# A recurrent layer whose operands are normalised ahead of its products, in token halves of 384 and 256

## The chip, the core and the metric

The kernel runs on one core of one Trainium2 chip. The metric is the device time of one execution in microseconds; the median of three runs of the kernel before is 1546.01 us (1545.75 to 1546.52). Engines are named as in the profile: PE (TensorE) with its weight loads PEld, DVE (VectorE), ACT (ScalarE), POOL (GpSimd) and SP, which issues most DMAs.

## The reference, cut to what matters

One step of a two-layer backbone over 512 latent tokens and 128 context tokens of width 1024, in float32. Layer 0 is attention and an FFN; layer 1 is a gated linear recurrent unit and an FFN. Every sub-layer starts with an RMS norm and a shift and scale that differ for latent and context tokens. The change touches the end of layer 0's FFN and the recurrent unit:

```
def _modulate(x, g, shift, scale):
    return _rms_norm(x, g) * (1 + scale[:, None, :]) + shift[:, None, :]

gate, xr = jnp.split(xm @ w_in, 2, axis=-1)           # two products, 1024 x 1024 each
xc = _centred_depthwise_conv(xr, conv_w, conv_b)      # 4 taps, zeros outside the sequence
a, b = _rglru_coeffs(xc, ...)                         # per direction: sigmoid, exp, sqrt
y = (scan_forward + scan_backward) * gelu(gate)
out = x + g * (y @ w_out)
```

## The kernel before, in words

Activations lie with features on the 128 partitions, eight feature tiles `k` by 640 tokens (512 latent tokens, stored column by column of the grid, then 128 context tokens). Each float32 operand is split into a rounded high part and a low part, and a product of one weight unit (eight 128x128 tiles, one output tile `f`) is three matmuls per `k`: hi x hi, hi x lo, lo x hi (`chunk`, lines 213 to 215). A product's result lies in one PSUM bank; the layer has three banks `mm` for them, and two pairs `gp` for the small gate products of line 1003.

**Last projection.** `project` multiplies for each `f` in token halves of 320, adds the result to the residual stream `x` (`residual`, L436), squares it for the statistics (L375, L377), and at once writes `x * A` as the next layer's operands `nh`, `nl` (`scale`, L419, L420): these are scaled but not normalised. After the last `f`, `stats` computes each token's mean square and its inverse root (`moment`: L389, L392, `var` L394, `rs` L396 on POOL, `dg` L398) and spreads it over the partitions (`spread`, L406), copied into `rt` (L430). `shift` puts the shift vector B into two further token columns, 640 and 641.

**Recurrent layer.** For each of eight feature tiles (columns, here) there are two products, `lru_xr` and `lru_gate`, in halves of 322 and 320 tokens (`CHB`): the two further columns give W B, copied to `bias` (L202). Eviction multiplies by `rt` on DVE (L981 for xr, written in row order of the grid; L1054 for the gate). Since W B is left to the bias, the pads of xr outside the sequence are filled with -bias (L973), and the convolution's constant `cbs` (L975) holds bias times the sum of taps. Then, per column, in the loop over `t` in `run`: `lru_a` (convolution L991, L993; small products L1003; tanh L1004; L1005), one step later `lru_b` (L1011; Exp L1015; tanh L1016; Sqrt L1017; L1018; L1019), one later `lru_c` (scans L1028; state L1030; sums L1035, L1036), and `lru_d` (gelu L1041; product with y L1042; high part L1046, low part L1047). A column takes three of ten buffers `lt` (`tr`, `ti`, `a`); `y` lives in `a`. The gate product of column f stands in the same step as its `lru_d`, but for column 0, which stands in the first step.

**What sets the order.** Engines run their own queues in order. Which instruction comes next on a queue is fixed at compile time by a planner: in a simulated run with its own costs, each engine takes the ready instruction that stands earliest in the program. Weights (`unit`): SP loads the float32 unit into one of three buffers `raw`; in the recurrent layer POOL loads it a second time straight into the high part `whi` (L178, three buffers), and DVE subtracts for `wlo` (L182). In the FFN phase there are three further buffers `whx`, `wlx`, and every second unit takes one of these. The output projection that follows (`project_halves`) needs the operands of all eight columns for its first product.

Of the kernel before, what the change touches and what calls it, by code (L numbers as in the profile page):

```python
# [9 lines left out]
F32 = mybir.dt.float32  # L10
F32R = mybir.dt.float32r
AF = mybir.ActivationFunctionType
# [113 lines left out]
class _Step:  # L126
# [313 lines left out]
    def project(self, w, hi, lo, gk, nxt=None, done=None, ahead=False):  # L440
        G = self.need(self.gcols, gk)
        for f in range(KT):
            u = self.unit(w[f], "m" if ahead else None)
            for t0, t1 in CH:
                self.residual(f, t0, t1, self.chunk(u, hi, lo, t0, t1, not ahead or f > 1), G, nxt)
                if nxt:
                    self.scale(f, t0, t1, *nxt)
            if done:
                done(f)
        if nxt:  # L450
            self.stats()
            self.shift(*nxt)

    def project_part(self, w, hi, lo, gk, also=None):
        G = self.need(self.gcols, gk)
# [465 lines left out]
    def lru_prep(self, pool):  # L921
        nc = self.nc
        c = CI["lam0"] * KT
        lam = self.t([P, 2 * KT], F32, "lam", 1, pool)
        nc.sync.dma_start(lam, self.i["cols"][:, c:c + 2 * KT])
        n = 2 * KT

        def sm(tag):
            return self.t([P, n], F32, tag, 1)
        ab = sm("l_ab")  # L930
        nc.vector.tensor_scalar(ab, lam, -1.0, None, ALU.mult)
        mx = sm("l_mx")
        nc.vector.tensor_scalar(mx, ab, 0.0, None, ALU.max)
        nc.vector.tensor_tensor(ab, ab, lam, ALU.min)
        y = sm("l_y")
        nc.scalar.activation(y, ab, AF.Exp)
        den = sm("l_den")
        nc.vector.tensor_scalar(den, y, 2.0, None, ALU.add)
        nc.vector.reciprocal(den, den)
        z = sm("l_z")  # L940
        nc.vector.tensor_tensor(z, y, den, ALU.mult)
        z2 = sm("l_z2")
        nc.vector.tensor_tensor(z2, z, z, ALU.mult)
        pl = sm("l_pl")
        nc.vector.memset(pl, 1.0 / 19)
        for c in range(17, 0, -2):
            nc.vector.tensor_tensor(pl, pl, z2, ALU.mult)
            nc.vector.tensor_scalar(pl, pl, 1.0 / c, None, ALU.add)
        nc.vector.tensor_tensor(pl, pl, z, ALU.mult)
        sp = sm("l_sp")  # L950
        nc.vector.scalar_tensor_tensor(sp, pl, 2.0, mx, ALU.mult, ALU.add)
        self.sp2 = sm("l_sp2")
        nc.vector.tensor_scalar(self.sp2, sp, 2.0, None, ALU.mult)
        self.sm4 = sm("l_sm4")
        nc.vector.tensor_scalar(self.sm4, sp, -4.0, None, ALU.mult)
        self.scw = self.t([P, KT], F32, "l_scw", 1)
        c = CI["cw0"] * KT
        nc.vector.tensor_reduce(self.scw, self.cols[:, c:c + 4 * KT].rearrange("p (j k) -> p k j", j=4), AX.X, ALU.add)
        self.hb = self.t([P, 4 * KT], F32, "l_hb", 1)
        c = CI["ba0"] * KT  # L960
        nc.vector.tensor_scalar(self.hb, self.cols[:, c:c + 4 * KT], 0.5, None, ALU.mult)

    def lru_xr(self, f, hi, lo, lp):
        nc = self.nc
        xr = self.t([P, 648], F32, "xr", 2, lp)
        nat = xr[:, 2:514].rearrange("p (r c) -> p c r", r=ROWS)

        def ev(t0, s, ps):
            if t0 == 0:
                todo = ((nat[:, 56:64], 0, 64, ROWS), (nat[:, 0:32], 64, 320, ROWS))  # L970
            else:
                for g, a, b in ((0, 0, 2), (0, 514, 515), (1, 515, 517), (1, 645, 646)):
                    nc.scalar.mul(xr[:, a:b], self.bias[:, g:g + 1].broadcast_to([P, b - a]), -1.0)  # L973
                self.cbs = self.t([P, 2], F32, "cbs", 2, lp)
                nc.vector.tensor_scalar(self.cbs, self.bias, self.scw[:, f:f + 1], self.col("cb", f), ALU.mult, ALU.add)  # L975
                todo = ((nat[:, 32:56], 320, 512, ROWS), (xr[:, 517:645], 512, 640, 0))
            for o, a, b, r in todo:
                v, w = ps[:, a - t0:b - t0], self.rt[:, a:b]
                if r:
                    v, w = [q.rearrange("p (c r) -> p c r", r=r) for q in (v, w)]  # L980
                nc.vector.tensor_tensor(o, v, w, ALU.mult)  # L981
        self.ws(self.i["wi"][KT + f], hi, lo, ev, ch=CHB)
        return xr, self.cbs

    def lru_a(self, f, xr, cbs, lp):
        nc = self.nc
        gw = self.t([P, 2, 2, P], F32, "gw", 2, lp)
        nc.sync.dma_start(gw, self.i["wg"][f])
        xc = self.t([P, LW], F32, "xc", 2, lp)
        for g, a, b in ((0, 0, NLAT), (1, NLAT, LW)):  # L990
            nc.scalar.activation(xc[:, a:b], xr[:, a:b], AF.Identity, scale=self.col("cw0", f), bias=cbs[:, g:g + 1])  # L991
        for j in range(1, 4):
            nc.vector.scalar_tensor_tensor(xc, xr[:, j:j + LW], self.col(f"cw{j}", f), xc, ALU.mult, ALU.add)  # L993

# [41 lines left out]
        nc.vector.tensor_tensor(y[:, NLAT:NTOK], h[:, 0, C0:LW], h[:, 1, C0:LW], ALU.add)  # L1036
        return y

    def lru_d(self, f, y, G, bias, yhi, ylo):
        for c, a, b in _pieces(0, NTOK):  # L1040
            self.nc.scalar.activation(G[:, a:b], G[:, a:b], AF.Gelu_apprx_tanh, bias=bias[:, c:c + 1])  # L1041
        self.nc.vector.tensor_tensor(y, y, G, ALU.mult)  # L1042
        self.split(yhi[:, f], ylo[:, f], y)

# [4 lines left out]
    def lru_gate(self, f, hi, lo, lp):  # L1049
        nc = self.nc  # L1050
        G = self.t([P, NTOK], F32, "gl", 3, lp)

        def ev(t0, s, ps):
            nc.vector.tensor_tensor(G[:, s], ps, self.rt[:, s], ALU.mult)  # L1054
        self.ws(self.i["wi"][f], hi, lo, ev, ch=CHB)
        return G, self.bias

    def new_x(self, st):
        pool = st.enter_context(self.tc.tile_pool(name="x", bufs=1))
# [6 lines left out]
    def run(self):  # L1066
# [65 lines left out]
        with self.phase("ffn0", at=2, rr=1, mx=2, wx=2, quota=56) as fp:  # L1132
            self.project(i["wo"], ohi, olo, (0, 2), ((0, 1), xhi, xlo), None, True)

            def last(w, hhi, hlo, gk):
                self.nh, self.nl = self.big(n=NTOK + 2), self.big(n=NTOK + 2)
                self.project(w, hhi, hlo, gk, ((1, 0), self.nh, self.nl),
                             lambda f: nc.sync.dma_start(xd[f * P:f * P + P], self.x[:, f]))
            self.ffn(0, xhi, xlo, fp, last)
        xpool.close()  # L1140
        mpool.close()
# [3 lines left out]
        ylo = self.big()  # L1145
        with self.phase("lru", at=1) as lp:
            A, B, C, G = {}, {}, {}, {}
            xr = self.lru_xr(0, xhi, xlo, lp)
            for t in range(KT + 2):
                if t < KT:  # L1150
                    A[t] = self.lru_a(t, *xr, lp)
                if t + 1 < KT:
                    xr = self.lru_xr(t + 1, xhi, xlo, lp)
                if 0 < t <= KT:
                    B[t - 1] = self.lru_b(t - 1, *A.pop(t - 1))
                if t > 1:
                    C[t - 2] = self.lru_c(t - 2, *B.pop(t - 2))
                g = 0 if t == 0 else t - 2
                if g > 0 or t == 0:
                    G[g] = self.lru_gate(g, xhi, xlo, lp)  # L1160
                if t > 1:
                    self.lru_d(t - 2, C.pop(t - 2), *G.pop(t - 2), yhi, ylo)
            nc.sync.dma_start(o["nh"], self.st)
        x1, x2 = self.big(n=NTOK + 2), self.big(n=NTOK + 2)
        self.new_x(self.ctx)
# [32 lines left out]
```

## Time and profile before

| | us |
|---|---|
| median of 3 runs (lowest, highest) | 1546.01 (1545.75, 1546.52) |
| the profiled execution | 1547.73 |
| its span, first to last instruction | 1546.0 |
| PE, DVE, ACT, POOL busy | 1492.0, 1069.5, 698.5, 215.9 |

Mean granted TensorE clock over the span: 0.988 of full speed. How to read it: PE's busy time is a union of modelled matmul spans, each longer than the distance to the next start, so short gaps don't show in it; DVE and ACT times are measured, and neighbouring instructions overlap by some 0.08 us. All times below are microseconds from the span's start unless marked ns. The last matmul of the last projection starts at 854.6, the recurrent layer's products begin at 855.1, and the output projection, which begins at 1025.6, waits before 1036.9.

### The profile page before, as it was taken

Reading aid. Unit: us, or ns where it says so; the run is one execution under the profiler, and the core shown is the slowest. Engines: PE = TensorE matmul, PEld = TensorE weight load, DVE = VectorE, ACT = ScalarE, POOL = GpSimd, SP = SyncE. Lnnn points to the kernel's source line nnn. Section 1 sums busy time; section 2 is a strip of 40 time slices with the busy share of each in tenths; the row PEclk is TensorE's granted clock in tenths of the full one; section 3 lists DMA queues with packets and bytes.
Section 4 is the critical chain, followed back from the end, with each engine's and each line's share of the span. In section 5 each row is a group of like instructions: output and inputs, shape, how many; then the busy total and the mean of one; then the engine's idle time right before and its main releaser. Section 6 shows DMA issues by size and latency. Waiting matters only on the chain. (4 is left out here: it accounts for less than half of the span.)

```text
span 1546.0 us, 26069 instructions
## 1 busy us (share of the span) xinstructions
PE 1492.0 (97%) x10315; PEld 1444.8 (93%) x10315; DVE 1069.5 (69%) x2034; ACT 698.5 (45%) x1304; POOL 215.9 (14%) x247
## 2 busy tenths in 40 slices
PE   6999999989999999999999999979999999999997
PEld 4899999879999999999999987869999999999996
DVE  5668788959998988443446479965875655555556
ACT  5576766655333113312324378762634342525242
POOL 2101122100111110000000000000222322222210
PEclk9999999999999999999999999989999999999998
DMA  9545656525566664222224433315242232323211
GB/s 373 151 117 162 188 165 174 154 105 186 190 193 192 188 208 140 62 82 82 65 73 133 131 115 106 103 55 201 79 130 82 83 96 69 96 69 93 72 56 68
DMA packets 72057, 196.64 MB, mean 127 GB/s; under 512 B 8048, under 2 KB 23552, under 8 KB 71808
## 3 DMA queue, kind: packets, MB, share of 16 engines
q1 hardware_dynamic: 57824, 144.49, 29.9%
q0 software_dynamic: 13824, 50.34, 10.8%
q8 instruction: 81, 1.33, 0.4%
q14 instruction: 40, 0.33, 0.1%
q10 hardware_dynamic: 288, 0.16, 0.0%
HBM read 179.48 MB, written 8.92 MB: 122 GB/s over the span
## 5 line engine op out<-in xcount | busy, mean ns | idle before, releaser
L213 PE MATMUL mm<-big,whi 128*128 128x320 f32 (+2 forms) x1290 | 402.8, 316 | 14.9 <-ACT big L1046 9.5
L214 PE MATMUL mm<-big,whi 128*128 128x320 f32 (+2 forms) x1290 | 405.6, 315 | 2.1 <-DVE big L1047 1.7
L215 PE MATMUL mm<-big,wlo 128*128 128x320 f32 (+2 forms) x1290 | 403.5, 314 | 0.7 <-DVE wlo L182 0.7
L213 PEld LDWEIGHTS mm<-big,whi 128*128 128x128 f32 x1290 | 245.3, 191 | 20.1 <-ACT big L1046 10.3
L214 PEld LDWEIGHTS mm<-big,whi 128*128 128x128 f32 x1290 | 246.5, 191 | 5.3 <-DVE big L1047 3.9
L215 PEld LDWEIGHTS mm<-big,wlo 128*128 128x128 f32 x1290 | 246.1, 191 | 2.2 <-DVE wlo L182 1.1
L243 DVE SCALAR_TENSOR_TENSOR mprod<-mraw,csb 128x1024 f32<-128x1024 f32 x160 | 195.6, 1223 | 14.6 <-DMA mraw<-in_wm 14.2
L436 DVE SCALAR_TENSOR_TENSOR x<-mm,G,x 128x128 f32<-128x128 f32 (+3 forms) x211 | 85.3, 434 | 86.1 <-PE mm L215 85.1
L182 DVE TENSOR_TENSOR wlo<-raw,whi 128x1024 fp32r<-128x1024 f32 (+1 forms) x90 | 110.5, 1228 | 33.4 <-ACT whi L180 21.1
L180 ACT CAST whi<-raw 128x1024 fp32r<-128x1024 f32 (+1 forms) x74 | 76.7, 1037 | 101.3 <-PE mm L214 69.6
L215 PE MATMUL mm<-big,wlx 128*128 128x320 f32 (+3 forms) x363 | 112.6, 310 | 0.0
L214 PE MATMUL mm<-big,whx 128*128 128x320 f32 (+3 forms) x363 | 112.3, 309 | 0.0
L213 PE MATMUL mm<-big,whx 128*128 128x320 f32 (+3 forms) x363 | 112.3, 309 | 0.0
L239 POOL DMA_DIRECT2D mraw<-in_wm x80 | 43.3, 542 | 385.0 <-DVE mprod L243 278.1
L213 PE MATMUL mx<-big,whi 128*128 128x320 f32 (+2 forms) x278 | 86.4, 311 | 0.9 <-DVE big L658 0.9
L215 PE MATMUL mx<-big,wlo 128*128 128x320 f32 (+2 forms) x278 | 86.1, 310 | 0.0
L214 PE MATMUL mx<-big,whi 128*128 128x320 f32 (+2 forms) x278 | 86.0, 309 | 0.0
L180 ACT CAST whx<-raw 128x1024 fp32r<-128x1024 f32 (+1 forms) x40 | 41.0, 1028 | 91.0 <-PE mm L214 53.3
L215 PE MATMUL mx<-big,wlx 128*128 128x320 f32 (+3 forms) x245 | 76.3, 311 | 0.0
L213 PE MATMUL mx<-big,whx 128*128 128x320 f32 (+3 forms) x245 | 76.1, 311 | 0.0
L214 PE MATMUL mx<-big,whx 128*128 128x320 f32 (+3 forms) x245 | 76.1, 311 | 0.0
L1046 ACT CAST whi<-raw 128x1024 fp32r<-128x1024 f32 (+1 forms) x41 | 41.3, 1008 | 71.3 <-PE mm L214 45.0
(292 smaller groups left out, 3589.0 us busy)
## 6 DMA issues: line engine op xcount, KB each, us to landing
raw<-in_gu SPq DMA_DIRECT2D x88, 512.0 KB, 3.6
mraw<-in_wm POOLq DMA_DIRECT2D x80, 512.0 KB, 4.0
raw<-in_dn SPq DMA_DIRECT2D x24, 512.0 KB, 3.6
raw<-in_wqk SPq DMA_DIRECT2D x16, 512.0 KB, 4.7
raw<-in_wi SPq DMA_DIRECT2D x16, 512.0 KB, 3.6
whi<-in_wi POOLq DMA_DIRECT2D x16, 512.0 KB, 3.9
raw<-in_dn SPq DMA_DIRECT2D x16, 448.0 KB, 3.4
sw<-in_wm SPq DMA_DIRECT2D x10, 512.0 KB, 10.4
```

The costliest lines, as they stand in the source:

```text
L180: nc.scalar.copy(hi, raw)
L182: nc.vector.tensor_tensor(lo, raw, hi.bitcast(F32), ALU.subtract)
L213: nc.tensor.matmul(ps, hi[:, k], xhi[:, k, s], start=(k == 0), stop=False)
L214: nc.tensor.matmul(ps, hi[:, k], xlo[:, k, s], start=False, stop=False)
L215: nc.tensor.matmul(ps, lo[:, k], xhi[:, k, s], start=False, stop=(k == nk - 1))
L239: nc.gpsimd.dma_start(w, self.i["wm"][l * 6 + j - 2, f])
L243: nc.vector.scalar_tensor_tensor(prod, w, 1.0, self.csb[:, s], ALU.mult, ALU.mult, accum_out=out[:, s, f:f + 1])
L436: self.nc.vector.scalar_tensor_tensor(xs, ps[:, a - t0:b - t0], G[:, s, f:f + 1], xs, ALU.mult, ALU.add)
L1046: self.nc.scalar.copy(hi, v)
```

## The change

- A new `project_closing` takes the place of `project` for the last projection of layer 0's FFN. All eight weight units are kept; the halves are 384 and 256 tokens (`CHL`). Tiles 0 and 1 are done in both halves, tiles 2 to 7 first in the first half alone. The statistics of the first half follow, then the second halves of tiles 2 to 7, and among them the first half is normalised, scaled, shifted and split (`modulate`: DVE, ACT, DVE for each piece); then the second half's statistics and the same for it. `x` is stored in two pieces per tile.
- The recurrent layer multiplies the normalised operands: no columns for B, no bias, no `rt`. xr is evicted by plain ACT copies; its pads are zeros, set once in two standing buffers; xc's first tap is one ACT instruction.
- The gate's first half is copied by ACT, its second half goes through gelu straight from PSUM, and the first half's gelu follows directly.
- The order at the start: first halves of xr 0, gate 0 and xr 1, then the second halves.

```diff
+    def project_closing(self, w, hi, lo, gk, key, nh, nl, xd):
+        G = self.need(self.gcols, gk)
+        A, B = [self.need(self.AB, key + (j,)) for j in range(2)]
+        us = []
+
+        def out(f, t0, t1):
+            self.residual(f, t0, t1, self.chunk(us[f], hi, lo, t0, t1), G, True)
+            self.nc.sync.dma_start(xd[f * P:f * P + P, t0:t1], self.x[:, f, t0:t1])
+
+        def normed(k, t0, t1):
+            v = self.t([P, 384], F32, "nv", 3, self.sb)
+            for s, a, b in _pieces(t0, t1):
+                self.modulate(k, a, b, A[:, s, k:k + 1], B[:, s, k:k + 1], v[:, a - t0:b - t0], nh, nl)
+        for f in range(KT):
+            us.append(self.unit(w[f]))
+            for c, (t0, t1) in enumerate(CHL):
+                if c == 0 or f < KT - DEH:
+                    out(f, t0, t1)
+        for c, (t0, t1) in enumerate(CHL):
+            for f in range(KT - DEH, KT) if c else ():
+                out(f, t0, t1)
+                j = f - KT + DEH
+                for k in range(max(0, 2 * j - 2), 2 * j) if f < KT - 1 else ():
+                    normed(k, *CHL[0])
+            self.stat(t0, t1)
+        for k in range(KT):
+            normed(k, *CHL[1])
...
+    def halves(self, w, hi, lo, ev):
+        u = self.unit(w)
+        return [lambda t0=t0, t1=t1: ev(t0, self.chunk(u, hi, lo, t0, t1)) for t0, t1 in CHL]
+
+    def lru_xr(self, f, hi, lo):
+        xr = self.xrs[f % 2]
         nat = xr[:, 2:514].rearrange("p (r c) -> p c r", r=ROWS)
-        def ev(t0, s, ps):
-            if t0 == 0:
-                todo = ((nat[:, 56:64], 0, 64, ROWS), (nat[:, 0:32], 64, 320, ROWS))
-            else:
-                for g, a, b in ((0, 0, 2), (0, 514, 515), (1, 515, 517), (1, 645, 646)):
-                    nc.scalar.mul(xr[:, a:b], self.bias[:, g:g + 1].broadcast_to([P, b - a]), -1.0)
-                self.cbs = self.t([P, 2], F32, "cbs", 2, lp)
-                nc.vector.tensor_scalar(self.cbs, self.bias, self.scw[:, f:f + 1], self.col("cb", f), ALU.mult, ALU.add)
-                todo = ((nat[:, 32:56], 320, 512, ROWS), (xr[:, 517:645], 512, 640, 0))
-            for o, a, b, r in todo:
...
-                nc.vector.tensor_tensor(o, v, w, ALU.mult)
+        def ev(t0, ps):
+            for o, a, b, r in ((nat[:, 56:64], 0, 64, ROWS), (nat[:, 0:40], 64, 384, ROWS),
+                               (nat[:, 40:56], 384, 512, ROWS), (xr[:, 517:645], 512, 640, 0)):
+                if t0 <= a and b <= t0 + 384:
+                    v = ps[:, a - t0:b - t0]
+                    self.nc.scalar.copy(o, v.rearrange("p (c r) -> p c r", r=r) if r else v)
+        return self.halves(self.i["wi"][KT + f], hi, lo, ev)
...
-        for g, a, b in ((0, 0, NLAT), (1, NLAT, LW)):
-            nc.scalar.activation(xc[:, a:b], xr[:, a:b], AF.Identity, scale=self.col("cw0", f), bias=cbs[:, g:g + 1])
+        nc.scalar.activation(xc, xr[:, 0:LW], AF.Identity, scale=self.col("cw0", f), bias=self.col("cb", f))
...
-    def lru_d(self, f, y, G, bias, yhi, ylo):
-        for c, a, b in _pieces(0, NTOK):
-            self.nc.scalar.activation(G[:, a:b], G[:, a:b], AF.Gelu_apprx_tanh, bias=bias[:, c:c + 1])
+    def lru_d(self, f, y, G, yhi, ylo):
         self.nc.vector.tensor_tensor(y, y, G, ALU.mult)
...
-        def ev(t0, s, ps):
-            nc.vector.tensor_tensor(G[:, s], ps, self.rt[:, s], ALU.mult)
-        self.ws(self.i["wi"][f], hi, lo, ev, ch=CHB)
-        return G, self.bias
+        def ev(t0, ps):
+            if t0 == 0:
+                nc.scalar.copy(G[:, 0:384], ps)
+                return
+            last = nc.scalar.activation(G[:, t0:NTOK], ps, AF.Gelu_apprx_tanh).ins
+            with self.tc.issue_after(last):
+                nc.scalar.activation(G[:, 0:t0], G[:, 0:t0], AF.Gelu_apprx_tanh)
+        return G, self.halves(self.i["wi"][f], hi, lo, ev)
...
-                self.project(w, hhi, hlo, gk, ((1, 0), self.nh, self.nl),
-                             lambda f: nc.sync.dma_start(xd[f * P:f * P + P], self.x[:, f]))
+                self.project_closing(w, hhi, hlo, gk, (1, 0), self.nh, self.nl, xd)
...
-            xr = self.lru_xr(0, xhi, xlo, lp)
+            self.xrs = [self.t([P, 648], F32, f"xr{j}", 1, lp) for j in range(2)]
+            for xr in self.xrs:
+                for a, b in ((0, 2), (514, 517), (645, 648)):
+                    nc.gpsimd.memset(xr[:, a:b], 0.0)
+
+            def gate(g):
+                G[g], halves = self.lru_gate(g, xhi, xlo, lp)
+                return halves
+            x0, g0, x1 = self.lru_xr(0, xhi, xlo), gate(0), self.lru_xr(1, xhi, xlo)
+            for step in (x0[0], g0[0], x1[0], x0[1], g0[1]):
+                step()
             for t in range(KT + 2):
                 if t < KT:
-                    A[t] = self.lru_a(t, *xr, lp)
+                    A[t] = self.lru_a(t, lp)
                 if t + 1 < KT:
-                    xr = self.lru_xr(t + 1, xhi, xlo, lp)
+                    for step in self.lru_xr(t + 1, xhi, xlo) if t else x1[1:]:
+                        step()
...
-                g = 0 if t == 0 else t - 2
-                if g > 0 or t == 0:
-                    G[g] = self.lru_gate(g, xhi, xlo, lp)
+                if t > 2:
+                    for step in gate(t - 2):
+                        step()
```

## Rows read from the trace of the kernel before

**Rows 1.** The page, part 1: busy us (share of the span) xinstructions.

```profile
PE 1492.0 (97%) x10315; PEld 1444.8 (93%) x10315; DVE 1069.5 (69%) x2034; ACT 698.5 (45%) x1304; POOL 215.9 (14%) x247
```

**Rows 2.** Stretches: us; busy (instructions) of PE, PEld, DVE, ACT, POOL; clock, DMA.

```profile
834.00:855.00 21.00, 21.00 (x145) 21.00 (x145) 12.63 (x27) 6.97 (x17) 1.05 (x2) 1.00 0.42 123
855.00:900.00 45.00, 43.82 (x278) 39.80 (x278) 19.78 (x38) 17.66 (x40) 3.88 (x6) 1.00 0.40 121
900.00:1003.00 103.00, 98.97 (x573) 85.85 (x572) 98.53 (x137) 84.38 (x136) 4.75 (x9) 0.98 0.36 110
1003.00:1028.00 25.00, 22.40 (x138) 21.59 (x137) 15.31 (x19) 22.34 (x27) 0.00 (x0) 0.93 0.16 44
1028.00:1041.00 13.00, 4.46 (x17) 3.80 (x16) 11.69 (x18) 2.71 (x7) 0.00 (x0) 0.67 0.11 38
```

**Rows 3.** Waits of PE, 855 to 1041: total us, times, longest us.

```profile
PE mm L213 <- ACT big L1046: 8.4, 1, 8.4
PE gp L1003 <- ACT lt L1004: 3.7, 3, 2.3
PE mm L213 <- DVE gl L1054: 2.9, 4, 1.9
```

**Rows 4.** Timeline of PE in the last product: start us, us, instruction.

```profile
1517.51 0.34 PE L215 MATMUL mm<-big,wlo 128*128 128x384 f32 x1
1517.68 0.28 PE L213 MATMUL mx<-big,whi 128*128 128x256 f32 x1
1517.80 0.28 PE L214 MATMUL mx<-big,whi 128*128 128x256 f32 x1
```

**Rows 5.** Groups by line, DVE, 860 to 1042: busy us, mean ns | idle before.

```profile
L182 DVE TENSOR_TENSOR wlo<-raw,whi 128x1024 fp32r<-128x1024 f32 x16 | 19.6, 1228 | 8.1 <-DMA whi<-in_wi 6.3 <-ACT whi L180 1.8
L981 DVE TENSOR_TENSOR xr<-mm,r 128x192 f32<-128x192 f32 (+3 forms) x32 | 10.8, 416 | 2.4 <-PE mm L215 2.4
L1054 DVE TENSOR_TENSOR gl<-mm,r 128x320 f32<-128x320 f32 x16 | 7.8, 499 | 0.7 <-PE mm L215 0.7
L975 DVE TENSOR_SCALAR cbs<-bias,l_scw,cols 128x2 f32<-128x2 f32 x8 | 2.3, 285 | 0.9 <-ACT bias L202 0.9
```

**Rows 6.** Groups by line, ACT, 860 to 1042.

```profile
L1041 ACT ACT_TABLE_LOAD x8 | 10.3, 1283 | 0.1
L1017 ACT ACT_TABLE_LOAD x8 | 10.3, 1283 | 0.1
L991 ACT ACTIVATE xc<-xr,cbs,cols 128x131 f32<-128x131 f32 (+1 forms) x16 | 9.8, 652 | 6.3 <-DVE xr L981 6.3
L973 ACT ACTIVATE xr<-bias 128x2 f32<-128x2 f32 (+1 forms) x32 | 3.8, 190 | 0.3 <-ACT r L430 0.2
L430 ACT COPY r<-rr 128x320 f32<-128x320 f32 x2 | 0.8, 425 | 4.9 <-PE rr L406 4.9
```

**Rows 7.** Groups by line and shape, DVE, 1490 to 1546 (the last projection of all).

```profile
L486 DVE SCALAR_TENSOR_TENSOR x<-x,cols,mx 128x384 f32<-128x384 f32 x8 | 4.5, 606 | 0.0
L436 DVE SCALAR_TENSOR_TENSOR x<-mm,G,x 128x128 f32<-128x128 f32 x10 | 3.1, 345 | 1.5 <-PE mm L215 1.5
L377 DVE TENSOR_TENSOR ssq<-ssq,sq 128x256 f32<-128x256 f32 x6 | 2.5, 422 | 1.3 <-ACT sq L375 1.1
```

**Rows 8.** Timeline of DVE at the statistics, 860 to 862.

```profile
860.20 0.23 DVE L394 TENSOR_SCALAR var<-at 128x3 f32<-128x3 f32 x2 [3.24 <-PE at L392]
861.42 0.56 DVE L398 TENSOR_TENSOR dg<-ident,rs 128x384 f32<-128x384 f32 x1 [0.99 <-POOL rs L396]
```

**Rows 9.** Timeline of DVE and of ACT at the layer's end.

```profile
1001.05 0.86 DVE L1047 TENSOR_TENSOR big<-lt,big 128x640 fp32r<-128x640 f32 x1
...
1023.60 1.50 DVE L1018 SCALAR_TENSOR_TENSOR lt<-lt,lt 128x1286 f32<-128x1286 f32 x1 [1.49 <-ACT bias L202]
...
1007.12 3.37 ACT L1015 ACTIVATE lt<-lt,l_sm 128x643 f32<-128x643 f32 x4
...
1010.40 0.78 ACT L1004 ACTIVATE lt<-gp,l_hb 128x643 f32<-128x643 f32 x1
```

More of the change, by code (lines that the diff above doesn't have):

```diff
@@ L955, in lru_prep @@
         nc.vector.tensor_scalar(self.sm4, sp, -4.0, None, ALU.mult)
-        self.scw = self.t([P, KT], F32, "l_scw", 1)
-        c = CI["cw0"] * KT
-        nc.vector.tensor_reduce(self.scw, self.cols[:, c:c + 4 * KT].rearrange("p (j k) -> p k j", j=4), AX.X, ALU.add)
         self.hb = self.t([P, 4 * KT], F32, "l_hb", 1)
@@ L961, in lru_prep, with lru_a @@
         nc.vector.tensor_scalar(self.hb, self.cols[:, c:c + 4 * KT], 0.5, None, ALU.mult)
-    def lru_xr(self, f, hi, lo, lp):
-        nc = self.nc
-        xr = self.t([P, 648], F32, "xr", 2, lp)
-        nat = xr[:, 2:514].rearrange("p (r c) -> p c r", r=ROWS)
-        def ev(t0, s, ps):
-            if t0 == 0:
-                todo = ((nat[:, 56:64], 0, 64, ROWS), (nat[:, 0:32], 64, 320, ROWS))
-            else:
-                for g, a, b in ((0, 0, 2), (0, 514, 515), (1, 515, 517), (1, 645, 646)):
-                    nc.scalar.mul(xr[:, a:b], self.bias[:, g:g + 1].broadcast_to([P, b - a]), -1.0)
-                self.cbs = self.t([P, 2], F32, "cbs", 2, lp)
-                nc.vector.tensor_scalar(self.cbs, self.bias, self.scw[:, f:f + 1], self.col("cb", f), ALU.mult, ALU.add)
-                todo = ((nat[:, 32:56], 320, 512, ROWS), (xr[:, 517:645], 512, 640, 0))
-            for o, a, b, r in todo:
-                v, w = ps[:, a - t0:b - t0], self.rt[:, a:b]
-                if r:
-                    v, w = [q.rearrange("p (c r) -> p c r", r=r) for q in (v, w)]
-                nc.vector.tensor_tensor(o, v, w, ALU.mult)
[L982 to L986, printed above, removed]
+    def halves(self, w, hi, lo, ev):
[3 more added lines that the diff above has]
+        xr = self.xrs[f % 2]
+        nat = xr[:, 2:514].rearrange("p (r c) -> p c r", r=ROWS)
+        def ev(t0, ps):
[5 more added lines that the diff above has]
+        return self.halves(self.i["wi"][KT + f], hi, lo, ev)
+    def lru_a(self, f, lp):
+        nc, xr = self.nc, self.xrs[f % 2]
         gw = self.t([P, 2, 2, P], F32, "gw", 2, lp)
@@ L1157, in run @@
                     C[t - 2] = self.lru_c(t - 2, *B.pop(t - 2))
-                g = 0 if t == 0 else t - 2
-                if g > 0 or t == 0:
-                    G[g] = self.lru_gate(g, xhi, xlo, lp)
+                if t > 2:
+                    for step in gate(t - 2):
+                        step()
                 if t > 1:
-                    self.lru_d(t - 2, C.pop(t - 2), *G.pop(t - 2), yhi, ylo)
+                    self.lru_d(t - 2, C.pop(t - 2), G.pop(t - 2), yhi, ylo)
             nc.sync.dma_start(o["nh"], self.st)
```

## The prediction

> **What bounds the kernel now.** I read the page's busy times first. TensorE is busy 97% of the span, VectorE 69%, ScalarE 45% [rows 1]: as a whole TensorE is the bound, and a change elsewhere pays only where TensorE stands still. So I looked next at the stage that the diff touches, by stretches [rows 2]. The end of the last projection (834 to 855) is dense. From 855 to 1003, the recurrent layer with all its columns in flight, TensorE is idle only 1.2 + 4.0 us. From 1003 to 1041, the end of the layer, it is idle 2.6 + 8.5 = 11.1 us, and the granted clock is 0.93 and 0.67 of full speed there, which costs about 0.07 x 22 + 0.33 x 4.5 = 3 us more. So some 19 us are to be had, of which 14 lie in the last 38 us.
>
> The list of waits [rows 3] says what ended them: 8.4 us the last yhi cast (the first product of the output projection needs all eight columns of y), 3.7 us a gate product waiting for ScalarE's tanh to empty its two banks, 2.9 us the eviction of a gelu-gate product by VectorE. Behind all three stands VectorE: between 900 and 1003 it is busy 98.5 of 103 us [rows 2], so the columns' chains run ever later than TensorE, and the debt is paid at the end. The timeline shows it: the x lo-part of one column (L1047) is finished only at 1001.9, the Exp of two columns comes as four in a row at 1007.12, with the last tanh behind them at 1010.40, and VectorE starts the last column's L1018 at 1023.60 [rows 9]. The ten lt buffers tie these together: a column takes three (tr, ti, a), so a late y (held until L1047) also holds up a later column's Exp, which needs a fresh one.
>
> **The change part by part.** *Products.* The rows of B (two columns more per unit) go, and the halves are 384 and 256. The profile has both: 0.17 us from a 384 to the next start, 0.12 us for a 256 [rows 4], 0.29 together; two of 320 took 2 x 21.00/143 = 0.29 us (145 records in the stretch, two of them cut) [rows 2]. 384 matmuls in the layer and 168 in the projection are split so: about nothing; between -1 and +1 us, I take -0.5.
>
> *VectorE in the columns.* It loses the four evictions of xr (10.8 us in all), the eviction of the gate product (7.8) and cbs (2.3) [rows 5]: 20.9 us, or some 16.5 when the 0.08 us by which neighbours overlap is taken off 56 times. That is 11 to 14% of the 145 us that it is busy from 855 to 1041 [rows 2]. Its load from 900 to 1003 falls from 96% to about 84%.
>
> *ScalarE in the columns.* It loses the eight groups of pads (3.8 us) and the tiny bias copies, and one of the two parts of xc (from 2 x 0.65 to about 0.95 for the whole, between 0.65 and 1.3) [rows 6]. It gains four xr copies: no row shows such a copy. From below, 640 elements at the pace of the contiguous PSUM copy of 320 in 0.425 us are 0.85; from above, VectorE's own price for the same four writes, 4 x 0.416 = 1.67 [rows 5, 6]; I take 1.3. The gate's first half is a new copy of 384, 0.5 us from the same row. The gelu keeps its 640 elements. Per column -0.5 - 0.35 + 1.3 + 0.5 = about +0.9 us, 7 us in all, with ends at 0 and 11. Between 900 and 1003 (some six columns) ScalarE goes from 84.4 to about 90 of 103 us [rows 2]: fuller, not full.
>
> *The joint.* Before, the products start on unnormalised operands and only the eviction waits for the statistics; that costs 1.2 us of TensorE [rows 2]. Now the first product needs the normalised first half. Count from T, when the last 384 half of the projection ends. TensorE has six second halves, 6 x 21 x 0.12 = 15.1 us [rows 4], and the small statistics matmuls, so it is free at T + 16. On VectorE: residual 0.6, then the statistics chain (var to the end of dg took 1.8 us [rows 8]) after square and matmuls, so the first modulate starts at about T + 5. It needs 8 x 2 instructions of 384, at 4.5/8 = 0.56 us each 9.0 us [rows 7]. Between them lie the residuals and sums of four second halves, 4 x (2 x 0.35 + 0.42) = 4.5 us [rows 7]: T + 18.5. The lo part of the first weight unit (L182, 1.23 us [rows 5]) stands behind them in program order, as its weight slot comes free only during the second halves, and the third matmul needs it: T + 20. So TensorE waits 2 us if the planner finds that split a gap, 4 if not; I take 3, and 1 us for the slower clock that follows such a gap (below), less the 1.2 that go: +2.5, with ends 0 and 6. The second half's modulate (8 x 4 instructions of 128 at about 0.32, 10 us [rows 7], from T + 22 or so) is covered by three products of 384, 3 x 24 x 0.17 = 12.2 us from T + 20: no wait left. The sixteen stores of x instead of eight queue on SP between weight loads whose buffers are three deep; the stores wait for residuals, the loads behind them have a product's time in hand; nothing. POOL issues the hi weights in slot order as before and the six memsets of the xr pads stand ahead of the first product's end; nothing.
>
> *The middle.* Of the 4.0 us idle, and about 2 us of clock (0.98 over 103 us), the waits for tanh stay in kind: ScalarE's order makes them. Those for VectorE's gate eviction go. -2 us, ends -5 and +5.
>
> *The end.* With VectorE at 84% the columns no longer fall behind, so the y of the earlier column is split and its lt buffers come free earlier, the Exp of the last two columns stop coming as a block of four, and the work of the last but one column leaves the run in which VectorE is busy 11.7 of the last 13 us [rows 2] with two columns at once. If all of that goes, the 14 us shrink to nearly nothing, as the three gate products left for the end (3 x 48 x 0.147 = 21 us) cover one column's chain. But the last chain keeps ScalarE's table loads and the planner's order, which nothing makes good. I take half: -7 us, ends 0 and -14.
>
> Sum: -0.5 + 2.5 - 2 - 7 = -7 us. The profiled execution took 1547.73 us with a span of 1546.0, so 1.7 us lie around the span; the median of the runs, 1546.01, is 1.7 below it. The change acts inside the span: 1539 for the median (some 1540.7 if profiled).
>
> **The rivals.** *Whole end recovered.* What is late next would be TensorE itself: -14 instead of -7, 1532, and with a smooth joint 1530. For it: VectorE is idle 9.7 of 25 us from 1003 to 1028, so it can do earlier work there. Against: ScalarE is busy 22.3 of 25 us from 1003 to 1028 [rows 2].
>
> *ScalarE takes over.* It now empties every bank of the layer, in order behind table loads of 1.28 us; eight for gelu and eight for sqrt stand in the profile [rows 6], besides the returns to tanh and Exp. A gelu forced at each product's end can cost one more return per column, 8 x 1.28 = 10.3 us, and the block of four Exp (3.4 us) then holds up an eviction. If half of it reaches TensorE: +5, 1544 (1540 to 1548). Against: three banks give a product's time of slack, and both gelu parts now run together, where before they sometimes had a load each. The Trainium skill, ScalarE: Activation LUTs (Table sets: the hidden batching unit), says to group calls by table set and not by function; the change goes against it, and the loads of this trace agree with it in size (1283 ns).
>
> *The joint takes it back (slower).* One mechanism: VectorE's queue holds the first unit's lo split behind the second half's modulate. Then TensorE waits not to T + 20 but to about T + 33, 13 us more than summed: 1552. It decides at one point: whether the first L182 of the layer stands on VectorE ahead of the first second-half modulate. For it: program order puts it behind. Against: the chain of the second statistics leaves VectorE a gap of some 3 us, in which a ready split fits.
>
> *It does not do what it says.* VectorE's 20 us were slack, the end is set by the chain through ScalarE and the scans, which all stay: -0.5 + 2.5, 1548.
>
> **How the numbers follow.** Forecast 0.45 (1533 to 1543 by itself), whole end 0.13 (1530), ScalarE 0.18 (1544), joint 0.14 (1552), nothing gained 0.10 (1548). A run of this kernel can tell about 0.2%, 3.1 us, from no change. Faster than 1542.9: 0.44 + 0.13 + 0.07 = 0.64. Within: 0.01 + 0.08 + 0.08 + 0.01 = 0.18. Slower than 1549.1: 0.13 + 0.03 + 0.02 = 0.18. The range leaves out the lower part of the second case (0.06) and most of the joint's (0.12): 1529 to 1551.
>
> **What would show it.** Right: VectorE at 80 to 88% in the 100 us after the first scan; TensorE idle at most 4 us between the projection and the first layer product; the wait for the last yhi cast down from 8.4 to about 4; no block of four Exp with a tanh behind it. Wrong: a wait over 8 us at the joint (the third rival), gl or xr evictions at ScalarE named as what TensorE waited for, more than 28 table loads in the layer (the second), or an unchanged 8 us at the end with VectorE idle in front of it (the last).

## The result, and the profile after

The change makes the kernel slower: median 1552.74 us (1550.93 to 1557.38, 8 runs) against 1546.26 for the kernel before in the same comparison, ratio 1.0043 (95% 1.0025 to 1.0061), or +6.5 us. The forecast was 1539 in a range of 1529 to 1551. The profiled execution took 1557.38 us, span 1555.6. Of that, 3.3 us lie ahead of the change, in code that it leaves alone (the first `rr` of the FFN starts at 399.99 instead of 396.65), so stretches are compared here, not spans.

The page, part 1, has VectorE down by 9.8 us and TensorE's work unchanged, as in [rows 1]:

```profile
PE 1491.8 (96%) x10309; PEld 1444.3 (93%) x10309; DVE 1059.7 (68%) x2000; ACT 698.2 (45%) x1282; POOL 216.9 (14%) x253
```

The stretches (columns as in [rows 2]): the joint, the hundred us in full flight, the last columns, the last chain.

```profile
860.00:905.00 45.00, 35.60 (x219) 33.73 (x218) 26.00 (x60) 18.55 (x41) 2.61 (x10) 0.89 0.37 121
912.00:1012.00 100.00, 93.70 (x540) 79.83 (x540) 83.87 (x96) 85.01 (x124) 5.38 (x9) 1.00 0.36 108
1012.00:1037.00 25.00, 22.08 (x150) 21.21 (x149) 16.91 (x18) 22.65 (x30) 0.00 (x0) 1.00 0.20 63
1037.00:1050.00 13.00, 6.73 (x38) 6.37 (x37) 11.89 (x19) 3.20 (x8) 0.00 (x0) 0.84 0.13 43
```

VectorE in full flight is at 84%, as forecast, from 96%. But TensorE stands 9.4 us in the joint, where it stood 1.2, and the granted clock is 0.89 there. The waits of PE, 855 to 1070 (compare [rows 3]):

```profile
PE mm L213 <- ACT xr L1001: 9.4, 1, 9.4
PE mm L213 <- ACT big L1062: 6.3, 1, 6.3
PE gp L1021 <- ACT lt L1022: 4.1, 4, 1.9
PE gp L1021 <- DVE xc L1011: 2.1, 1, 2.1
PE mm L213 <- ACT gl L1073: 2.0, 1, 2.0
PE mm L213 <- ACT gl L1071: 0.9, 1, 0.9
```

The first line is new, and larger than the whole loss. The second is the stop for the last yhi cast (8.4 before). The gate evictions by VectorE are gone (2.9), but ScalarE's copy and gelu now cost 2.9, and a convolution that comes late (xc) 2.1.

To compare kernels I summed, over all records of PE's timeline, the distance from one matmul's start to the next less what that shape takes undisturbed (0.176 us for 384 columns, 0.119 for 256, 0.149 for 320 or 322, 0.429 for the 512 columns of the small products, 0.112 for their other 131 and for the statistics). It counts stops and slow clock together, in us, from the one profile of each kernel:

| | joint | full flight | end | sum, less before | median, less before |
|---|---|---|---|---|---|
| before | 1.3 | 6.4 | 16.4 | | |
| after | 11.6 | 7.8 | 12.4 | +7.7 | +6.5 |
| e1_stat_early | 7.5 | 7.8 | 12.6 | +3.8 | +2.1 |
| e2_xr_outside | 7.5 | 8.2 | 9.7 | +1.3 | +0.5 |
| e3_both | 2.3 | 8.6 | 12.1 | -1.1 | -1.4 |
| e4_evac_dve | 11.6 | 7.5 | 16.7 | +11.7 | +11.3 |
| e9_gate_later | 2.1 | 7.5 | 7.1 | -7.4 | -5.5 |
| e11_before_gate_later | 1.3 | 5.5 | 11.5 | -5.8 | -4.8 |

(Joint: from the projection's end, some 45 us; end: from some 35 us ahead of the matmul that waited for the last yhi cast to 15 behind it. The column of medians is from each comparison's own runs.)

**The joint, read in the timelines.** PE, the layer's first matmul, the second half's statistics and the stop:

```profile
860.68 0.34 PE L213 MATMUL mm<-big,whi 128*128 128x384 f32 x1
...
869.11 0.28 PE L389 MATMUL at<-ones,ssq 128*128 128x1 f32 x2
...
874.26 0.61 PE L406 MATMUL rr<-dg,ones 128*128 128x128 f32 x4
884.27 0.58 PE L213 MATMUL mm<-big,whi 128*128 128x256 f32 x1 [9.40 <-ACT xr L1001]
884.65 0.41 PE L214 MATMUL mm<-big,whi 128*128 128x256 f32 x1
884.86 0.41 PE L215 MATMUL mm<-big,wlo 128*128 128x256 f32 x1
```

ACT's last square, and its first eviction of xr:

```profile
862.88 0.42 ACT L375 ACTIVATE sq<-x 128x256 f32<-128x256 f32 x1 [0.63 <-DVE x L436]
...
883.40 0.81 ACT L1001 COPY xr<-mm 128x64 f32<-128x64 f32 x2 [0.66 <-DVE big L413]
```

DVE around them (L411 and L413 are the first and last part of `modulate`):

```profile
851.08 1.23 DVE L182 TENSOR_TENSOR wlo<-raw,whi 128x1024 fp32r<-128x1024 f32 x1 [0.57 <-DMA whi<-in_wi]
...
863.23 1.22 DVE L182 TENSOR_TENSOR wlo<-raw,whi 128x1024 fp32r<-128x1024 f32 x1
...
864.89 0.42 DVE L377 TENSOR_TENSOR ssq<-ssq,sq 128x256 f32<-128x256 f32 x1
...
866.52 1.15 DVE L413 SCALAR_TENSOR_TENSOR big<-nv,B,big 128x384 fp32r<-128x384 f32 x2 [0.16 <-ACT big L412]
870.10 0.16 DVE L394 TENSOR_SCALAR var<-at 128x2 f32<-128x2 f32 x1 [2.43 <-PE at L392]
...
874.90 1.64 DVE L411 SCALAR_TENSOR_TENSOR nv<-x,A,rr 128x128 f32<-128x128 f32 x6 [3.33 <-PE rr L406]
...
882.20 1.13 DVE L413 SCALAR_TENSOR_TENSOR big<-nv,B,big 128x128 fp32r<-128x128 f32 x4
```

POOL, the zeroing of xr's pads:

```profile
883.44 0.27 POOL L1170 MEMSET xr<- 128x2 f32 x6 [12.31 <-DVE big L413]
```

Two things meet. First, the last square is done at 863.3 and the last sum that the statistics read (L377) at 865.31, yet their matmuls start at 869.11: the planner put them deep in the three interleaved products of 384 columns, and `rr` at their very end, 2.7 us behind `dg` (done at 871.57 on VectorE). VectorE, done with the first half at 867.7, had nothing but the short statistics until 874.9. Second, ScalarE's first eviction and POOL's zeroing both start right behind VectorE's last L413, which writes neither xr nor its bank; it reads nv, a tile of the FFN's memory pool, which closes where the layer's opens. xr is the first tile written in the layer's pool, and the program makes the first write there wait for the last instruction on the pools closed before it (e2 below tests this). Three products had their results in the three `mm` banks and none could be emptied; TensorE had nowhere to write.

### The profile page after: what moved, and what is told of

It is laid out like the page before. It is cut to its first block, busy times and chain, and to the rows that moved or that the text cites. A ratio compares the mean times of both kernels' runs of the same rounds, so it can differ in the third digit from the quotient of the medians.

```text
span 1555.6 us, 26009 instructions
## 1 busy us (share of the span) xinstructions
PE 1491.8 (96%) x10309; PEld 1444.3 (93%) x10309; DVE 1059.7 (68%) x2000; ACT 698.2 (45%) x1282; POOL 216.9 (14%) x253
## 5 line engine op out<-in xcount | busy, mean ns | idle before, releaser
L213 PE MATMUL mm<-big,whi 128*128 128x320 f32 (+3 forms) x1290 | 402.4, 315 | 21.3 <-ACT xr L1001 9.4
L214 PE MATMUL mm<-big,whi 128*128 128x320 f32 (+3 forms) x1290 | 404.8, 314 | 0.7 <-DVE big L1063 0.4
L215 PE MATMUL mm<-big,wlo 128*128 128x320 f32 (+3 forms) x1290 | 404.0, 314 | 0.7 <-DVE wlo L182 0.7
L182 DVE TENSOR_TENSOR wlo<-raw,whi 128x1024 fp32r<-128x1024 f32 (+1 forms) x90 | 110.1, 1223 | 29.8 <-ACT whi L180 21.6
L213 PE MATMUL mx<-big,whi 128*128 128x320 f32 (+3 forms) x278 | 86.5, 311 | 0.9 <-DVE big L686 0.9
L214 PE MATMUL mx<-big,whi 128*128 128x320 f32 (+3 forms) x278 | 86.3, 310 | 0.0
L215 PE MATMUL mx<-big,wlo 128*128 128x320 f32 (+3 forms) x278 | 86.3, 310 | 0.0
```

What stands on the lines that cost most here:

```text
L182: nc.vector.tensor_tensor(lo, raw, hi.bitcast(F32), ALU.subtract)
L213: nc.tensor.matmul(ps, hi[:, k], xhi[:, k, s], start=(k == 0), stop=False)
L214: nc.tensor.matmul(ps, hi[:, k], xlo[:, k, s], start=False, stop=False)
L215: nc.tensor.matmul(ps, lo[:, k], xhi[:, k, s], start=False, stop=(k == nk - 1))
```

## The experiments

My theory after the result was that both orders are at fault and each costs several us; the rivals, that one of them does it all, and that the rest of the forecast gain is missing for a reason of its own. All times are medians; "less before" is against the kernel before in the same comparison (1547.06 for e1 to e4, 1547.47 for e5 to e8, 1546.86 for e9 to e11). The kernel after was measured against 1546.26, so a difference to it is given against before as well.

**e1_stat_early** pins the second half's sums and their spread earlier among the 72 matmuls of the three products (`issue_after` keeps what is in its block behind the named instruction):

```diff
-            for step in (x0[0], g0[0], x1[0], x0[1], g0[1]):
+            for step, pin in ((x0[0], {3: self.at, 5: self.rr}), (g0[0], {3: self.at, 5: self.rr}), (x1[0], {3: self.at, 5: self.rr}), (x0[1], {}), (g0[1], {})):
+                self.pin = pin
                 step()
-            nc.tensor.matmul(ps, hi[:, k], xhi[:, k, s], start=(k == 0), stop=False)
+            with self.tc.issue_after(pin[k]) if k in pin else nullcontext():
+                nc.tensor.matmul(ps, hi[:, k], xhi[:, k, s], start=(k == 0), stop=False)
```

> Only TensorE's order at the joint changes: the second half's statistics matmuls (at) are pinned after 27 of the 72 matmuls of the three first-half products, the spreading ones (rr) after 45. In the changed kernel they came after 53 and after all 72, at 869.1 and 874.3, though the squares were ready at 863.3. Theory A (the 9.4 us wait at the joint is the second half's normalisation starting late, because its statistics stand late in TensorE's queue): rr at about 868.5, the last low part of the normalisation at about 877 instead of 883.3, the wait 3 to 5 us, the time 5 to 6 us below the changed kernel, near 1547. Rival B (the wait is VectorE's throughput, two instructions per piece): the first half's normalisation ends at 867.7 and the second's 8.5 us follow whenever statistics come, so also an earlier end, but only if VectorE was idle before; under B alone, without idle time to use, no change. Rival C (the loss is in the columns, ScalarE's evictions): 1552, unchanged.

Measured 1549.19, ratio 1.0014 (1.0004 to 1.0023). The sums start 5.1 us behind the projection's last matmul (8.6 after), the spread 9.2 (13.7), and the stop on PE is halved and still ends with the same line:

```profile
879.98 0.58 PE L216 MATMUL mm<-big,whi 128*128 128x256 f32 x1 [4.63 <-ACT xr L1004]
```

So the late statistics are worth some 4 us (4.1 in the joint by the table; against before, +6.5 becomes +2.1), and they are not all of it.

**e2_xr_outside** leaves the order and takes the first xr buffer from a slot of the standing pool:

```diff
-            self.xrs = [self.t([P, 648], F32, f"xr{j}", 1, lp) for j in range(2)]
+            self.xrs = [self.t([P, 648], F32, "r", 1), self.t([P, 648], F32, "xr1", 1, lp)]
```

> The first of the two standing xr buffers is taken from the long-lived pool (the place of the r vector), the other stays in the layer's pool; nothing else. Theory A2 (the first eviction of the layer waits for the last instruction on the closed pools, VectorE's last low part of the normalisation, and with three banks full TensorE can't go on): the first xr eviction comes at about 866 instead of 883.4, a bank is free, and the first second-half product runs paced by the normalisation; the wait named ACT xr goes, and the stop of 9.4 us falls to about 6.5 spread over pieces, 3 us less time, near 1549.5. Rival B2 (TensorE waits for the second half's operands, which come as late as the bank): the wait changes its name only, under 1 us gained. Rival C: unchanged.

Measured 1547.51, ratio 1.0000 (0.999 to 1.001), 5.2 us less than after (against before, +6.5 becomes +0.5). ACT now empties the first bank as soon as its product ends, 11.2 us behind the projection's last matmul where it was 22.8 after, while the gate's first copy, whose target still lies in the layer's pool, waits for the last L413 as before:

```profile
868.24 0.85 ACT L1001 COPY r<-mm 128x64 f32<-128x64 f32 x2 [4.71 <-PE mm L215]
...
879.82 0.48 ACT L1071 COPY gl<-mm 128x384 f32<-128x384 f32 x1 [0.66 <-DVE big L413]
```

and PE goes on, now at the pace of the normalisation itself (in step with VectorE's pieces), the statistics as late as after:

```profile
870.67 0.60 PE L406 MATMUL rr<-dg,ones 128*128 128x128 f32 x4
872.44 0.38 PE L213 MATMUL mm<-big,whi 128*128 128x256 f32 x1 [1.17 <-ACT big L412]
873.53 0.39 PE L214 MATMUL mm<-big,whi 128*128 128x256 f32 x1 [0.71 <-DVE big L413]
```

The wait on the closed pools is shown: a slot elsewhere takes it away for one tile, and it stays for the other. The gain in the joint is 4.1 us by the table. The other 2.7 are at the end, where this kernel's list of waits has no line for gl at all (2.9 in after and in e1): the same copy and the same direct gelu, in another order of ScalarE.

**e3_both** is both edits.

> Both edits of the joint together: statistics pinned early and the first xr buffer outside the layer's pool. Theory A + A2: the stop at the joint falls to 0 to 2 us, the time is 8 to 9 us below the changed kernel, 1543.5 to 1545, that is 1 to 3 us below the kernel before, since its end of the layer is some 5 us shorter. Rival B (throughput): a stop of 5 us or more stays. Rival C: unchanged near 1552.

Measured 1545.63, ratio 0.9990 (0.9982 to 0.9999): 7.1 us less than after (against before, +6.5 becomes -1.4). In the joint the two edits add up: they are worth 9.3 us by the table, and 4.1 each alone. The joint and full flight:

```profile
858.00:893.00 35.00, 33.88 (x215) 31.38 (x215) 25.75 (x60) 17.95 (x41) 2.74 (x7) 1.00 0.46 148
893.00:1001.00 108.00, 100.97 (x577) 85.59 (x575) 87.42 (x99) 89.14 (x130) 5.90 (x10) 1.00 0.37 110
```

The joint's stop is gone, with the clock at 1.00. But against before only 1.4 us are won, at the edge of what can be told; the next runs ask where the rest is.

**e4_evac_dve** is after with the evictions of xr and gate on VectorE again, gelu late in two parts.

```diff
-                    self.nc.scalar.copy(o, v.rearrange("p (c r) -> p c r", r=r) if r else v)
+                    self.nc.vector.tensor_copy(o, v.rearrange("p (c r) -> p c r", r=r) if r else v)
...
+            nc.vector.tensor_copy(G[:, t0:384 if t0 == 0 else NTOK], ps)
```

> The changed kernel with the evictions of xr and of the gate product as VectorE copies and the gelu back in the last step of a column, in parts of 512 and 128: VectorE carries again about what it carried before, ScalarE less. The joint is untouched (its stop stays at 9 to 10 us). Theory D (the lighter VectorE shortened the layer's end): TensorE's idle time from the last gate products to the output projection grows back from 10 to 14 or 16 us, VectorE is over 95% busy in the 100 us before it, and the time rises to 1556 or more. Rival E (the end got shorter by the planner's order, not by VectorE's load): the end stays at 10 to 12 us and the time at 1552. Rival C (ScalarE's evictions cost TensorE time in the columns, the four waits for gl of 3.2 us and those for tanh): the time falls by 3 to 5 us.

Measured 1558.38, ratio 1.0069 (1.0057 to 1.0081), 5.6 us more than after (against before, +6.5 becomes +11.3), with the joint as in after and the end at 16.7 instead of 12.4. VectorE is busier, though not by as much as I expected:

```profile
915.00:1015.00 100.00, 95.43 (x550) 81.83 (x549) 91.37 (x123) 78.15 (x99) 4.75 (x9) 0.98 0.35 111
```

Moving the evictions off VectorE is worth some 4 us at the end, as the sign of the prediction's last term has it. This run moves the gelu too; the next two take the edits apart.

**e5_xr_dve** is e3 with the four xr copies alone on VectorE (the first change of the diff above); **e6_gelu_late** is e3 with two plain copies of the gate and one gelu of 640 in `lru_d`:

```diff
-            last = nc.scalar.activation(G[:, t0:NTOK], ps, AF.Gelu_apprx_tanh).ins
-            with self.tc.issue_after(last):
-                nc.scalar.activation(G[:, 0:t0], G[:, 0:t0], AF.Gelu_apprx_tanh)
+            nc.scalar.copy(G[:, t0:384 if t0 == 0 else NTOK], ps)
...
+        self.nc.scalar.activation(G, G, AF.Gelu_apprx_tanh)
```

> On the version with both edits of the joint (median 1545.6), the four xr evictions go back to VectorE as copies; the gate product stays on ScalarE with direct gelu. Theory D (VectorE's load sets how late the columns run): VectorE rises from 83% to about 88 or 90% in the 100 us of full flight, the stop before the output projection grows by 1 to 3 us, the time is 1546.5 to 1548.5. Rival C (ScalarE's evictions cost more than VectorE's would): the waits for gl of 2.9 us and for tanh of 4.9 us shrink, the time falls to 1542 to 1544.

> On the same version, both halves of the gate product are evicted by plain ScalarE copies and one gelu of 640 elements stands in the column's last step, as before. Theory F (the direct gelu makes TensorE wait, because a bank is emptied only after a table load and in the order that the planner gave it): the waits for gl at the last two gates (2.9 us) fall under 1 us, and the time falls by 1 to 3 us, to 1543 to 1545. Rival G (a copy more per column costs ScalarE 0.4 us and brings the gelu later onto the chain of y): the end grows, the time rises by 1 to 3 us.

Measured 1548.40, ratio 1.0006 (0.9997 to 1.0015), and 1546.27, ratio 0.9989 (0.9980 to 0.9998). ScalarE's xr copies are a gain of some 2.5 us, not a cost. The way is not the one that I expected: in e5 VectorE is busy 90.7 of the 100 us from 905 to 1005 (85.4 in e3), but the stop for the last cast is 3.6 instead of 6.2; the waits for gl are 6.0 instead of 2.9, and the end by the table is 14.9 instead of 12.1. The direct gelu is worth nothing that can be told: in e6 the waits for gate evictions fall from 2.9 to 1.3, and the time does not.

**e7_lt12** (on e3) and **e8_before_lt12** (on the kernel before) have twelve buffers `lt` in place of ten:

```diff
-NLT = 10
+NLT = 12
```

> On the same version, twelve lt buffers instead of ten. Theory H (the ring of lt buffers, three per column, holds up the Exp of the last columns, so that a late y delays them): the stop before the output projection falls from 8.5 by 2 to 5 us, the time to 1541 to 1544. Rival I (the end is the last column's own chain through tanh, Exp, Sqrt, two scans and the split, with the order of ScalarE): under 1 us of change.

> The kernel before with twelve lt buffers instead of ten, nothing else. Theory H: the block of four Exp at 1007 falls apart, the Exp of the last column but one comes some 5 to 8 us earlier, and the idle time at the end (16 us with the slower clock) falls by 3 to 7 us: 1540 to 1544. Rival D (VectorE's load alone makes the end late, buffers don't matter): under 1 us of change, 1546.5 to 1547.5.

Measured 1545.51, ratio 0.9985 (0.9976 to 0.9994), and 1547.51, ratio 0.9997 (0.9988 to 1.0007): neither differs from its base. The Exp block still comes as four, in e7 at 1002.92 for 3.38 us. The buffers are not what ties the last columns.

**e9_gate_later** (e3 with twelve `lt`) moves each gate product and its `lru_d` one loop step later, so that four gate products instead of three stand behind the last small products; **e10_gate_late_gelu_late** adds the late gelu of e6; **e11_before_gate_later** makes the same move in the kernel before, also with twelve `lt`.

```diff
-            for t in range(KT + 2):
+            for t in range(KT + 3):
...
-                if t > 1:
+                if 1 < t < KT + 2:
                     C[t - 2] = self.lru_c(t - 2, *B.pop(t - 2))
+                if t > 3:
+                    for step in gate(t - 3):
+                        step()
                 if t > 2:
-                    for step in gate(t - 2):
-                        step()
-                if t > 1:
-                    self.lru_d(t - 2, C.pop(t - 2), G.pop(t - 2), yhi, ylo)
+                    self.lru_d(t - 3, C.pop(t - 3), G.pop(t - 3), yhi, ylo)
```

> On the version with both edits of the joint and twelve lt buffers (median 1545.5), the gate product and the last step of a column come one loop step later, so four gate products instead of three are left for TensorE after the last small products. Theory K (the 6.4 us stop before the output projection is the last column's chain of some 37 us, which 21 us of gate products don't cover; 7 us more of product there cover it, if the steps before stand it): the stop falls to 0 to 2 us, the waits in the columns grow by at most 2 us, the time falls to 1540 to 1543. Rival L (the columns, with less product per step, wait for VectorE and ScalarE instead, so the 7 us come back as waits for tanh and for xc): the waits in the columns grow by 5 us or more, the time is 1544.5 to 1547.

> The same with both halves of the gate product evicted by plain copies and one gelu in the column's last step. If theory F (direct gelu makes TensorE wait for banks) holds, 1 us or more below the version with the gate later alone; if G (longer chain of y), no faster than it.

> The kernel before with the gate product and the last step of a column one loop step later and twelve lt buffers. Theory M (VectorE's load is what keeps the kernel before late; moving a product does not take work off it): little gain, 1545.5 to 1547.5, the waits in the columns grow by what the end gains. Rival K alone (the uncovered chain at the end is all): a gain of 4 us or more, 1542 to 1543, as large as on the changed kernel.

Measured 1541.40, ratio 0.9960 (0.9947 to 0.9972); 1544.09, 0.9982 (0.9973 to 0.9991); 1542.07, 0.9965 (0.9952 to 0.9979). e9 is the best kernel here and beats both before and after. Its waits of PE, 855 to 1070, have the last yhi cast at 2.5 in place of 6.2 in e3:

```profile
PE gp L1024 <- ACT lt L1025: 5.2, 4, 2.3
PE mm L216 <- ACT big L1065: 2.5, 1, 2.5
PE mm L216 <- ACT gl L1076: 1.3, 1, 1.3
```

and those of e11 at 5.3 in place of 8.4, with VectorE's evictions still in it:

```profile
PE mm L213 <- ACT big L1046: 5.3, 1, 5.3
PE gp L1003 <- ACT lt L1004: 3.4, 5, 0.9
PE mm L213 <- DVE gl L1054: 3.0, 3, 1.9
```

The end lacked products to cover the last chain, and these can be had without the change: -4.8 us from an edit of the loop (e8 shows that the two further buffers alone give nothing; the gate product and `lru_d` were not moved apart from each other). In e10 the late gelu takes back 2.7 of e9's 5.5 us: the stop for the last cast is 6.7 again. So with late gates the direct gelu is worth something, where in e6 it was worth nothing. Whether e9 is better than e11, that is whether the change still adds something once the order is right, these runs can't say: the intervals overlap.

## Why the prediction was wrong

**The failed step is the joint**: "The second half's modulate [...] is covered by three products of 384 [...] no wait left", and "POOL issues the hi weights [...] and the six memsets [...] nothing". I priced the joint at +2.5 (0 to 6; its terms, 3 + 1 - 1.2, are 2.8); by the table it is +10.3. Counted from T, here 843.7, the second half's modulate was to start at T + 22 and end at T + 32; it starts at T + 31 (874.90) and ends at T + 40. The cover was there in length (860.68 to 874.26, against 8.4 us of modulate) but I counted only what VectorE does and not where on TensorE's queue the second half's sums would stand, and not what the first eviction waits for; the memsets, put at nothing, wait for the same L413. The three products also fill the three banks, so the cover ends at their end unless ScalarE can empty one. e3 repairs both: the joint costs 2.3, +1.0 over before, below what I had summed. The gap that I did price, 3 us ahead of the layer's first product, did not come: its first matmul follows the projection's last within 0.12 us (860.68), though the first half's modulate ends only at 867.7, since the matmuls take the feature tiles one by one as they come. The 1 us for the slower clock was 2.0, behind a stop at another place.

**VectorE's order at the joint was right**, and with it the named rival's mechanism was wrong though its time, 1552, was nearly met. Its point of decision was whether the layer's first L182 stands on VectorE ahead of the first second-half modulate: it does, at 851.08 (the third at 863.23) against 874.90, and the first three products ran without a stop. Its sign, a wait over 8 us at the joint, and the second rival's, an xr eviction by ScalarE named as what TensorE waited for, did both come, but from another cause: ScalarE was not too full there (busy 18.6 of the 45 us from 860), it waited.

**VectorE's load was right** (84% forecast, 83.9 measured). **ScalarE's additions were right in size**: four xr copies per column at 1.3, measured 1.35. These are the groups by line and shape of ACT, 860 to 1055:

```profile
L1009 ACT ACTIVATE xc<-xr,cols 128x643 f32<-128x643 f32 x8 | 7.4, 923 | 2.0 <-DVE lt L1023 1.7
L1001 ACT COPY xr<-mm 128x320 f32<-128x320 f32 x8 | 6.0, 746 | 0.0
...
L1001 ACT COPY xr<-mm 128x128 f32<-128x128 f32 x16 | 4.0, 357 | 6.3 <-PE mm L215 6.2
L1071 ACT COPY gl<-mm 128x384 f32<-128x384 f32 x8 | 3.8, 471 | 0.0
...
L1001 ACT COPY xr<-mm 128x64 f32<-128x64 f32 x8 | 2.2, 272 | 1.5 <-PE mm L215 0.9 <-DVE big L413 0.7
```

The three groups of L1001 are 12.2 us, 10.8 as one group without the overlaps of neighbours, and 10.8/8 = 1.35. The rival of more table loads fell: there are 21 in the layer against 24, one fewer each for gelu (8 to 7), Sqrt (8 to 7) and Exp (5 to 4). The Trainium skill, ScalarE: Activation LUTs (Table sets: the hidden batching unit), which the rival cited, writes about 2.7 us beside each load; the 1283 ns with which the rows agree is that page's figure for the load by itself (What ACT_TABLE_LOAD costs). No run here puts its advice to batch by set to the test.

**The middle had the wrong sign**: -2 forecast, +1.4 by the table. The term took the waits for VectorE's gate eviction out of the middle, but of their 2.9 us only 0.3 lay there; the rest lay at the end, as PE's timeline before shows:

```profile
956.09 0.41 PE L213 MATMUL mm<-big,whi 128*128 128x320 f32 x1 [0.29 <-DVE gl L1054]
...
1013.90 0.41 PE L213 MATMUL mm<-big,whi 128*128 128x320 f32 x1 [1.86 <-DVE gl L1054]
```

What the middle got instead is the wait for xc, 2.1 us, which ends at 988.61: on VectorE the last part of a convolution (L1011) stands behind the next step of another column (L1036), which itself waits for ScalarE:

```profile
986.26 1.50 DVE L1036 SCALAR_TENSOR_TENSOR lt<-lt,lt 128x1286 f32<-128x1286 f32 x1 [1.36 <-ACT lt L1035]
987.68 0.88 DVE L1011 SCALAR_TENSOR_TENSOR xc<-xr,cols,xc 128x643 f32<-128x643 f32 x1
```

At the end the waits for VectorE's gate eviction did go, but ScalarE's order makes as many. In its timeline the gate copy stands behind a block of Exp, and the gelu behind three tanh, a cast and a table load:

```profile
1015.19 3.38 ACT L1033 ACTIVATE lt<-lt,l_sm 128x643 f32<-128x643 f32 x4
...
1019.96 0.46 ACT L1071 COPY gl<-mm 128x384 f32<-128x384 f32 x1
1020.32 2.56 ACT L1034 ACTIVATE lt<-lt,l_sp 128x643 f32<-128x643 f32 x3
...
1023.84 1.28 ACT L1073 ACT_TABLE_LOAD   x1
1025.13 0.38 ACT L1073 ACTIVATE gl<-mm 128x256 f32<-128x256 f32 x1
```

TensorE's two stops for gl end at 1020.48 and 1025.57, each 0.06 behind the end of such a row. It is the second rival's mechanism, at 2.9 us in place of 5, and it hangs on the order: e2, with the same instructions, has no such wait.

**The end was right in sign and near in size**: -7 forecast (0 to -14), -4.0 by the table; e4, which takes VectorE's relief back, loses 4.3 there. Two of its reasons fell. The Exp still come as a block of four (row at 1015.19), and more buffers don't change it (e7, e8); that it is the planner's order is likely, but was not tried. And the last two columns still go through VectorE together, so that it is as full in the last 13 us (11.89) as before (11.69 in [rows 2]):

```profile
1028.55 2.91 DVE L1036 SCALAR_TENSOR_TENSOR lt<-lt,lt 128x1286 f32<-128x1286 f32 x2 [1.77 <-ACT lt L1035]
...
1045.75 1.57 DVE L1058 TENSOR_TENSOR lt<-lt,gl 128x640 f32<-128x640 f32 x2
1047.38 1.56 DVE L1063 TENSOR_TENSOR big<-lt,big 128x640 fp32r<-128x640 f32 x2
```

Even with a sound joint (e3, where it costs +1.0) the change is worth -1.4 us; without the joint that is -2.4, where the other terms made -9.5. That e2 is 1.7 us faster than e1 with the same joint fits the waits for gl (2.9 us) that e2 lacks at the end. Left open: why the planner places the sums so late, and why its order at the end differs between e1 and e2 (its costs were not varied).

## What to carry to other kernels

When a phase's first results come while the phase before still works, ask what the first write into the new memory waits for, and give the tiles that are needed early a place in a pool that stays open. A product covers a wait only as long as there is a free bank for the next one, and only if the small matmuls that feed the wait stand early in TensorE's own queue: look where the order puts them. Taking evictions off a full engine shortened the end here by some 4 us (e4); a product moved behind other products, so that it runs beside the last chain, was worth as much (4.8, e11) and cost one edit of a loop.

## What the runs showed of the hardware

- A ScalarE copy took longer where its writes are scattered. The copy of 128x320 whose neighbouring elements land 64 floats apart takes 746 ns; the contiguous ones out of PSUM take 425 for 320 [rows 6] and 471 for 384. The Trainium skill, SBUF — State Buffer (Door 1: The DMA port swizzle), says that accesses that leave a 16-byte line pay a penalty; the trace agrees with the direction, and the ratio here is 746/425 = 1.76.
- A stop of TensorE had a second price. After the 9.4 us the 256-column matmuls stand 0.213 us apart (rows from 884.27) until 888.70, then 0.119 again: some 21 x 0.094 = 2.0 us. The granted clock is 0.50 from 884.27 to 888.70, the lower of its two levels (1.2 GHz), and 1.00 from there to 905. The same followed shorter stops in e2: after four of 0.4 to 1.2 us (3.2 in all) it is 0.50 from 877.03 to 882.86. In e3, where no stop of the joint is over 0.5 us, the granted clock stays at 1.00.
